# Sixteen weight tiles of a hybrid decoder layer: their low parts made by accumulating DMAs in place of VectorE subtractions

## The chip, the cores and the metric

The kernel runs on one core of one Trainium2 chip. The metric is the device time of one execution in microseconds, as the median of its runs; less is better. Engines are named as in the profile: PE (TensorE matmul), PEld (TensorE weight load), DVE (VectorE), ACT (ScalarE), POOL (GpSimd) and SP (SyncE). POOL and SP matter here as queues that issue DMAs: POOL's DMAs run on the queue that the profile calls q0 software_dynamic, SP's on q1 hardware_dynamic.

## What is computed

One layer of a decoder trunk for 512 positions and a model width of 1024, in float32:

```
u = RMSNorm(x);  z = u @ w_in            # columns: MoBA q,k,v | mLSTM q,k | mLSTM v | output gate | i,f gates | branch gates A, B
A = block-sparse causal attention (8 heads x 64)
B = chunkwise mLSTM (4 heads x 128), normalised, times sigmoid(output gate)
m = sigmoid(z_gA) * (A @ w_proj_a) + sigmoid(z_gB) * (B @ w_proj_b)
x = x + m @ w_out
x = x + SwiGLU(RMSNorm(x)) @ w_down;  out = RMSNorm(x)
```

Two families of weights are touched here: the branch gate B columns of w_in (called "gb") and the two projections w_proj_a and w_proj_b (called "p").

## The kernel before, in words

All products are made in three matmul passes, to keep float32 accuracy on a faster reduced format (float32r). A weight tile w is split into a high part h, which is w rounded to float32r, and a low part l = w - h. The same is done to the activations. Then h·h, l·h and h·l are accumulated in PSUM (`mm3`, lines 194 to 203): three matmuls for each 128 rows of depth, so 24 for one tile of 128 by 1024.

The weights ahead of the feed-forward part come as 60 such tiles, in the order of the table `UNITS`: q, k, v and mLSTM tiles first, then numbers 28 to 35 "ga" (branch gate A), 36 to 43 "gb" (branch gate B), 44 to 51 "p" (the projections, A and B rows side by side) and 52 to 59 "wo" (w_out). The helper `fill` takes the next tile and issues its matmuls, and between tiles the code issues the matmuls of attention and mLSTM. Two helpers prepare the tiles:

- `load_pair` (line 180) issues the loads of two tiles on SP's queue into buffers "raw" (pool tag R, 7 buffers; two of these hold activations until the last gb tile is done, so 5 rotate).
- `split_unit` (line 188) takes one raw tile and calls `split_hl` (line 157): ACT rounds it into "wh" (line 148) and DVE subtracts into "wl" (line 161). Both buffers come from pool tag W (10 buffers, two of them held as above). A raw buffer is free after the subtraction, a W buffer after the last matmul of its tile.

`fill` keeps the splits two tiles ahead of the matmuls. After the first stage the order of instructions on each engine is set by the scheduler that builds the program, from priorities and its own estimates; every engine then runs its list strictly in order, and each queue issues its DMAs in order.

Three more pieces come up later. The projections' outputs wait in 3 PSUM buffers "mm"; those of ga and gb are taken out by DVE (`run_g`, line 575), and the next tile that gets the same buffer can't start before that. The mLSTM part loads, for each of its 4 heads, a tile "R" of decay rows from DRAM on POOL's queue (`ml_load`, line 1370); DVE (line 1382) and ACT work on it next. And the feed-forward part issues 22 accumulating loads on POOL's queue (`gu_load`, line 705), which add DRAM data to a tile in SBUF, and 32 accumulating stores to DRAM (line 921).

The functions that the change touches, and what calls them:

Of the kernel before, what the change touches and what calls it, by code (L numbers as in the profile page):

```python
# [9 lines left out]
F32R = mybir.dt.float32r  # L10
BF16 = mybir.dt.bfloat16
AF = mybir.ActivationFunctionType
ALU = mybir.AluOpType
# [37 lines left out]
def _unit_order():  # L51

    u = []
    u += [("q", 0), ("q", 1), ("k", 0), ("k", 1), ("q", 2), ("q", 3)]
    u += [("va", 0), ("va", 1), ("va", 2), ("va", 3), ("k", 2), ("k", 3)]
    u += [("ob", 0), ("ob", 1)]
    u += [("vb", i) for i in range(4)]
    for h in (0, 2):
        u += [("qkb", h), ("qkb", 4 + h), ("qkb", h + 1), ("qkb", 5 + h)]
    u += [("ob", 2), ("ob", 3)]  # L60
    u += [("ga", m) for m in range(8)]
    u += [("gb", m) for m in range(8)]
    u += [("p", m) for m in range(8)]
    u += [("wo", m) for m in WO]
    return u


UNITS = _unit_order()
# [16 lines left out]
def hybrid_layer_kernel(ctx: ExitStack, tc, xT, wall, wgu, wds, wdl, g3v, vecs, wgates, consts, rope, out):  # L85
    nc = tc.nc
# [12 lines left out]
    def nm(p="t"):  # L99
        cnt[0] += 1  # L100
        return f"{p}{cnt[0]}"

    def slot(dt=F32, name="a"):
        return act.tile([P, S], dt, name=nm(name), tag="A")
# [4 lines left out]
    def blk(dt=F32, name="b", raw=False):  # L109
        t = dict(tag="R", bufs=NR) if raw else dict(tag="W", bufs=NW)  # L110
        return act.tile([P, 2 * S], dt, name=nm(name), **t)
# [16 lines left out]
    f = lambda t: t.bitcast(F32)  # L128
# [6 lines left out]
    def table(set_id):  # L135
        if ph["set"] == set_id:
            return
        with ExitStack() as es:
            for i in ph["ins"]:
                es.enter_context(tc.issue_after(i))  # L140
            ld = A.add_instruction(
                mybir.InstLoadActFuncSet(name=nc.get_next_instruction_name(), act_func_set_id=set_id)
            )
        ph.update(set=set_id, load=raw_ins(ld), ins=[])

    def act_(out_, in_, func, **kw):
        if func not in SETS:
            return A.activation(out_, in_, func, **kw)  # L148
        table(SETS[func])
        if ph["manual"]:  # L150
            return A.activation(out_, in_, func, **kw)
        with tc.issue_after(ph["load"]):
            i = A.activation(out_, in_, func, **kw)
        ph["ins"].append(raw_ins(i))
        return i

    def split_hl(src, name="h", dst=None):

        h, l = dst or (slot(F32R, name + "h"), slot(F32R, name + "l"))
        act_(h, src, AF.Copy)  # L160
        V.tensor_tensor(l, src, f(h), op=ALU.subtract)  # L161
        return h, l
# [11 lines left out]
    raw = {}  # L174
    whl = {}
# [4 lines left out]
    def load_pair():  # L180
        p = wstate["pair"]
        if p * 2 >= NU:
            return
        for u in (2 * p, 2 * p + 1):
            raw[u] = blk(name="raw", raw=True)
            nc.sync.dma_start(raw[u], wall[u])
        wstate["pair"] += 1

    def split_unit():
        u = wstate["split"]  # L190
        wstate["split"] += 1
        whl[u] = split_hl(raw.pop(u), dst=(blk(F32R, "wh"), blk(F32R, "wl")))
        if u % 2 == 1:
            load_pair() if u < NGEN - 4 else st["load"]()

# [33 lines left out]
    wstate["pair"] = 2  # L229
    wstate["split"] = 4  # L230
    load_pair()
    con = cst.tile([P, NC_], F32, name="con")
    nc.sync.dma_start(con, consts)
# [43 lines left out]
    for k in range(KT):  # L277
        if k < 4:
            t = blk2(F32R, "u", raw=k < 2)
            h, l = t[:, 0, :], t[:, 1, :]  # L280
        else:
            h, l = slot(F32R, "uh"), slot(F32R, "ul")
        wh, wl = w0h[k // 4][:, k % 4], w0l[k // 4][:, k % 4]
        halves = [(0, 1), (2, 3)] if k == 0 else [range(4)]
        c = slice(0, P * len(halves[0]))
        split_hl(t0[k // 4][:, k % 4, c], dst=(wh[:, c], wl[:, c]))
        act_(h, xs[k], AF.Copy, scale=col(G1 + k))
        V.scalar_tensor_tensor(l, xs[k], col(G1 + k), f(h), op0=ALU.mult, op1=ALU.subtract)
        uh.append(h)
        ul.append(l)  # L290

        for js in halves:
            if js[0]:
                c = slice(2 * P, S)
                split_hl(t0[0][:, 0, c], dst=(wh[:, c], wl[:, c]))
            for n, (w, r) in enumerate(((wh, h), (wl, h), (wh, l))):
                for j in js:
                    T.matmul(ps0[j], w[:, j * P : (j + 1) * P], r, start=k == 0 and n == 0, stop=k == KT - 1 and n == 2)  # L298
        if k:
            add_sq(1, xs[k - 1], k - 1)  # L300
        if k == KT - 4:
            load_pair()
        if k >= KT - 3:
            split_unit()
        if k == KT - 2:
            split_gw()
# [58 lines left out]
    def fill(n=1, mid=None):  # L365

        for _ in range(n):
            u = pos[0]
            if u >= len(UNITS):
                if mid:  # L370
                    mid()
                return
            while wstate["split"] <= min(u + LOOK, NGEN - 1):
                split_unit()
            pos[0] += 1
            kind, i = UNITS[u]
            g = run[kind](i, *whl.pop(u))
            next(g, None)
            if mid:
                mid()  # L380
            for _ in g:
                pass
# [1006 lines left out]
    def ml_a(h, b):  # L1389
        qh, ql = qkm[h]  # L1390
        kh, kl = qkm[4 + h]
        res = []
        for i in ((0, 1), (2,))[b]:
            ps = mmb() if i == 1 else sb()
            w = rbc[h][i]
            n = w.shape[-1]
            for j in range(4):
                if KR[j][0] == i:
                    c = slice(j * P, (j + 1) * P)
                    o = ps[:, KR[j][1]]  # L1400
                    T.matmul(o, kh[:, c], qh[:, j * P :], start=True, stop=False)
                    T.matmul(o, kl[:, c], qh[:, j * P :], start=False, stop=False)
                    T.matmul(o, kh[:, c], ql[:, j * P :], start=False, stop=True)
            V.scalar_tensor_tensor(w, ps[:, :n], sc_b, w, op0=ALU.mult, op1=ALU.mult)
            h_, l_ = slot(F32R, "Ah"), slot(F32R, "Al")
            res.append(split_hl(w, dst=(h_[:, :n], l_[:, :n])))

        w0, w1, w2 = rbc[h][0:3]
        if b == 0:
            V.tensor_tensor(w0[:, P:], w0[:, P:], w1, op=ALU.add)  # L1410
        else:
            V.tensor_tensor(w0[:, 2 * P :], w0[:, 2 * P :], w2[:, 0:256], op=ALU.add)
            V.tensor_tensor(w0[:, 3 * P :], w0[:, 3 * P :], w2[:, 256:384], op=ALU.add)
            res.append(split_hl(w0, "D"))
        return res, lambda: None
# [72 lines left out]
    while n < len(steps) or qa or qb:  # L1488
        if qa and (len(qa) >= LA or n >= len(steps)):
            kind, h, b, r = qa.pop(0)  # L1490
            qb.append((kind, h, b, moba_b(h, b, r) if kind == "a" else r, n))
        if n < len(steps):
            kind, h, b = steps[n]
            while kind == "b" and not (h in wready and h in qkm and 4 + h in qkm):
                advance()
            r, second = moba_a(h, b) if kind == "a" else ml_a(h, b)
# [22 lines left out]
        while qb and (qb[0][4] <= n - LC):  # L1519
            kind, h, b, r, _ = qb.pop(0)  # L1520
# [115 lines left out]
```

## Time and profile before

| what | value |
| --- | --- |
| median of 3 runs | 733.04 us (733.04 to 733.22) |
| profiled execution, first to last instruction (span) | 730.5 us |
| median less this span: what lies around it (the page gives no other time of its own for the profiled execution) | 2.5 us |
| PE busy | 721.6 us (99% of the span) |
| DVE busy | 618.7 us (85%) |
| ACT busy | 430.6 us (59%) |
| POOL busy | 64.6 us (9%) |
| granted TensorE clock, mean | 0.996 |

The profile is one execution, taken by the hardware profiler. Times inside it count from the first instruction. A row of a group of instructions has the busy time, the mean duration of one, and the idle time of the engine just before them with what ended it. PE's matmuls are pipelined, so the start of the next matmul tells more than the end of one.

### The profile page before, as it was taken

What the parts mean: (1) busy time and instruction counts of PE and PEld (TensorE: products, weight loads), DVE (VectorE), ACT (ScalarE), POOL (GpSimd) and SP (SyncE); (2) the same over time, 40 slices, a digit from 0 to 9 for tenths busy, and PEclk for the clock granted to TensorE, in tenths of its full rate; (3) what the DMA queues carried; (4) which work ended last, traced back from release to release, by engine and by line L of the source; (5) the groups of instructions that cost most, each with busy time, mean ns of one, the idle gap of its engine ahead of it and who ended that gap; (6) DMA issues with size and microseconds to landing.
All of it is one profiled execution on the core that took longest, in us unless ns stands there. A gap on an engine that the chain in (4) does not pass through costs nothing.

```text
span 730.5 us, 11386 instructions
## 1 busy us (share of the span) xinstructions
PE 721.6 (99%) x4191; PEld 636.7 (87%) x4191; DVE 618.7 (85%) x1106; ACT 430.6 (59%) x748; POOL 64.6 (9%) x87
## 2 busy tenths in 40 slices
PE   9999999999999999999999999999999999999995
PEld 6788888888888888888888998999899899899984
DVE  6998877899987669566788999899899899989996
ACT  6635776668846339523456656665655565655554
POOL 0004010000000000000000000400310310130000
PEclk9999999999999999999999999999999999999998
DMA  8778673232431222534767353975895795696403
GB/s 308 280 229 222 186 214 118 73 131 91 162 136 58 87 87 87 173 112 118 190 175 208 121 160 95 237 220 131 207 266 144 173 273 161 150 247 203 151 0 117
DMA packets 51320, 118.74 MB, mean 163 GB/s; under 512 B 5292, under 2 KB 9780, under 8 KB 51264
## 3 DMA queue, kind: packets, MB, share of 16 engines
q1 hardware_dynamic: 37024, 88.82, 35.9%
q0 software_dynamic: 9728, 26.80, 19.2%
q10 hardware_dynamic: 4512, 2.39, 1.1%
q8 instruction: 33, 0.54, 0.3%
q14 instruction: 23, 0.19, 0.1%
HBM read 101.17 MB, written 16.82 MB: 162 GB/s over the span
## 4 chain that ended last, share of the span: by engine, by line
PE 98%; DVE 0%; DMA 0%; issue 0%; ACT 0%; SPq 0%
PE mm L201 12%; PE mm L202 12%; PE mm L203 12%; PE mm L795 6%; PE mm L796 6%; PE mm L797 6%; PE s L795 3%; PE s L797 3%; PE s L796 3%; PE mm L904 3%; PE mm L905 2%; PE mm L906 2%; PE acc L1351 2%; PE mm L298 2%; PE mm L479 2%; PE mm L480 2%
## 5 line engine op out<-in xcount | busy, mean ns | idle before, releaser
L148 ACT ACTIVATE wh<-raw 128x1024 fp32r<-128x1024 f32 x56 | 59.2, 1058 | 77.7 <-PE mm L202 73.5
L795 PE MATMUL mm<-bq,w 128*128 128x256 f32 x264 | 75.6, 286 | 0.0
L796 PE MATMUL mm<-bq,w 128*128 128x256 f32 x264 | 74.9, 284 | 0.0
L797 PE MATMUL mm<-bq,w 128*128 128x256 f32 x264 | 74.8, 283 | 0.0
L161 DVE TENSOR_TENSOR wl<-raw,wh 128x1024 fp32r<-128x1024 f32 x56 | 68.1, 1219 | 6.4 <-ACT wh L148 5.5
L743 DVE TENSOR_TENSOR w<-s,w 128x1024 fp32r<-128x1024 f32 x44 | 53.6, 1218 | 8.4 <-ACT w L148 8.4
L148 ACT ACTIVATE w<-s 128x1024 fp32r<-128x1024 f32 x44 | 46.5, 1056 | 14.5 <-PE mm L202 5.4
L148 ACT ACTIVATE w<-raw 128x1024 fp32r<-128x1024 f32 (+2 forms) x48 | 46.1, 963 | 12.7 <-PE s L796 3.3
L705 POOL DMA_DIRECT2D s<-in_wgu_dram x22 | 19.0, 865 | 368.5 <-DVE ga L597 131.8
L795 PEld LDWEIGHTS mm<-bq,w 128*128 128x128 f32 x264 | 50.6, 192 | 0.7 <-ACT s L148 0.3
L796 PEld LDWEIGHTS mm<-bq,w 128*128 128x128 f32 x264 | 50.6, 192 | 0.3 <-issue 0.2
L797 PEld LDWEIGHTS mm<-bq,w 128*128 128x128 f32 x264 | 50.6, 192 | 0.1
L201 PE MATMUL mm<-u,wh 128*128 128x512 f32 x128 | 50.4, 394 | 0.0
L202 PE MATMUL mm<-u,wl 128*128 128x512 f32 x128 | 50.1, 391 | 0.0
L203 PE MATMUL mm<-u,wh 128*128 128x512 f32 x128 | 50.0, 391 | 0.0
L797 PE MATMUL s<-bq,w 128*128 128x256 f32 x176 | 49.8, 283 | 0.0
L202 PE MATMUL mm<-uh,wl 128*128 128x512 f32 x128 | 49.8, 389 | 0.0
L201 PE MATMUL mm<-uh,wh 128*128 128x512 f32 x128 | 49.8, 389 | 0.0
L203 PE MATMUL mm<-ul,wh 128*128 128x512 f32 x128 | 49.8, 389 | 0.0
L795 PE MATMUL s<-bq,w 128*128 128x256 f32 x176 | 49.8, 284 | 0.0
L796 PE MATMUL s<-bq,w 128*128 128x256 f32 x176 | 49.8, 283 | 0.0
L148 ACT ACTIVATE w<-sw 128x1024 fp32r<-128x1024 f32 x20 | 21.2, 1059 | 22.2 <-DVE sw L782 20.2
(404 smaller groups left out, 2238.2 us busy)
## 6 DMA issues: line engine op xcount, KB each, us to landing
raw<-in_wall_dram SPq DMA_DIRECT2D x56, 512.0 KB, 4.1
s<-in_wgu_dram SPq DMA_DIRECT2D x22, 512.0 KB, 4.8
s<-in_wgu_dram POOLq DMA_DIRECT2D x22, 512.0 KB, 5.9
raw<-in_wgu_dram SPq DMA_DIRECT2D x22, 512.0 KB, 5.2
raw<-in_wds_dram SPq DMA_DIRECT2D x20, 512.0 KB, 5.5
w<-in_wgu_dram SPq DMA_DIRECT2D x22, 256.0 KB, 6.8
h1d<-s POOLq DMA_DIRECT2D x16, 256.0 KB, 8.7
R<-scr POOLq DMA_DIRECT2D x4, 896.0 KB, 4.7
```

The lines of the kernel that those rows point to most:

```text
L148: return A.activation(out_, in_, func, **kw)
L161: V.tensor_tensor(l, src, f(h), op=ALU.subtract)
L201: T.matmul(ps, wh[:, c], rh[j], start=start and j == 0, stop=False)
L202: T.matmul(ps, wl[:, c], rh[j], start=False, stop=False)
L203: T.matmul(ps, wh[:, c], rl[j], start=False, stop=stop and j == n - 1)
L298: T.matmul(ps0[j], w[:, j * P : (j + 1) * P], r, start=k == 0 and n == 0, stop=k == KT - 1 and n == 2)
L705: nc.gpsimd.dma_start(s13, wgu[i][:, 512:1536].rearrange("p (x c) -> p x c", x=2), accum_op=ALU.add)
L743: V.tensor_tensor(dst[1], src, f(dst[0]), op=ALU.subtract)
L795: T.matmul(ps, wh[:, c], bh, start=first and k == 0, stop=False, skip_group_check=not first)
L796: T.matmul(ps, wl[:, c], bh, start=False, stop=False, skip_group_check=not first)
L797: T.matmul(ps, wh[:, c], bl, start=False, stop=k == 3, skip_group_check=not first)
L904: T.matmul(ps, bh, wh[:, d], start=first and k == 0, stop=False, skip_group_check=not first)
```

## The change

For the eight gb tiles, the load moves from SP to POOL and writes a float32r tile, so that the transfer itself rounds ("rawh", in the R buffers); this is used as the high part. ACT writes the negated high part into wl, and a second DMA on POOL adds the same weights from DRAM to it. For the eight p tiles, the load stays on SP; ACT makes the high part and, in a second pass, the negated one, and a DMA on POOL adds the raw tile from SBUF to that. The 16 subtractions on DVE are gone. The other tiles are as before. Line numbers from 193 on move by 19.

```diff
--- before
+++ after
@@ load_pair @@
         for u in (2 * p, 2 * p + 1):
-            raw[u] = blk(name="raw", raw=True)
-            nc.sync.dma_start(raw[u], wall[u])
+            kind = UNITS[u][0]
+            if kind == "gb":
+                raw[u] = blk(F32R, "rawh", raw=True)
+                nc.gpsimd.dma_start(raw[u], wall[u])
+            else:
+                raw[u] = blk(name="raw", raw=True)
+                nc.sync.dma_start(raw[u], wall[u])
@@ split_unit @@
-        whl[u] = split_hl(raw.pop(u), dst=(blk(F32R, "wh"), blk(F32R, "wl")))
+        kind = UNITS[u][0]
+        if kind == "gb":
+            h, l = raw.pop(u), blk(F32R, "wl")
+            act_(l, f(h), AF.Copy, scale=-1.0)
+            nc.gpsimd.dma_start(l, wall[u], accum_op=ALU.add)
+            whl[u] = h, l
+        elif kind == "p":
+            r, h, l = raw.pop(u), blk(F32R, "wh"), blk(F32R, "wl")
+            act_(h, r, AF.Copy)
+            act_(l, r, AF.Copy, scale=-1.0)
+            nc.gpsimd.dma_start(l, r, accum_op=ALU.add)
+            whl[u] = h, l
+        else:
+            whl[u] = split_hl(raw.pop(u), dst=(blk(F32R, "wh"), blk(F32R, "wl")))
```

The scheduler puts the instructions into a new order. The first place is POOL's list in the mLSTM stage: R is the tile of decay rows, one for each of the four heads, in_wall_dram holds the weight tiles, and s is a tile of the feed-forward part. Before:

```order
L1370 DMA R_1765<-scr 128x1792
L1370 DMA R_2048<-scr 128x1792
L1370 DMA R_2125<-scr 128x1792
L1370 DMA R_2288<-scr 128x1792
L705 DMA s_3563<-in_wgu_dram 128x1024
```

After the change:

```order
L1389 DMA R_2125<-scr 128x1792
L188 DMA rawh_2464<-in_wall_dram 128x1024
L188 DMA rawh_2466<-in_wall_dram 128x1024
L188 DMA rawh_2575<-in_wall_dram 128x1024
L1389 DMA R_2288<-scr 128x1792
L188 DMA rawh_2577<-in_wall_dram 128x1024
L188 DMA rawh_2679<-in_wall_dram 128x1024
L202 DMA wl_2626<-in_wall_dram 128x1024
```

The loads of the first three gb tiles now stand between the third and the fourth R load, on the same queue.

The second place is POOL's list further down, with the accumulating transfers (line 202 for gb, 208 for p) of the last gb tiles and the first p tiles; there was nothing here before:

```order
L188 DMA rawh_2681<-in_wall_dram 128x1024
L202 DMA wl_2880<-in_wall_dram 128x1024
L188 DMA rawh_2793<-in_wall_dram 128x1024
L202 DMA wl_2920<-in_wall_dram 128x1024
L188 DMA rawh_2795<-in_wall_dram 128x1024
L202 DMA wl_2954<-in_wall_dram 128x1024
L208 DMA wl_2995<-raw_2883 128x1024
L208 DMA wl_3032<-raw_2885 128x1024
L208 DMA wl_3069<-raw_2957 128x1024
```

The loads of gb tiles 5, 6 and 7 alternate with accumulating transfers, each of which waits for ACT.

The third place is ACT's list at the end of the mLSTM stage (ri, ob and yb belong to the mLSTM output, sqh to its norm, ga and gb are the gates). Before:

```order
L148 ACTIVATE sqh_2779<-sqn_2772 128x512
L148 ACTIVATE wh_2885<-raw_2683 128x1024
L148 ACTIVATE wh_2926<-raw_2797 128x1024
L153 ACTIVATE ri_2864<-d_2667 128x512
L153 ACTIVATE ri_2864<-ri_2864 128x512
L153 ACTIVATE ri_2877<-d_2773 128x512
L153 ACTIVATE ri_2877<-ri_2877 128x512
L141 ACT_TABLE_LOAD
```

After the change:

```order
L148 ACTIVATE sqh_2776<-sqn_2769 128x512
L148 ACTIVATE wl_2880<-rawh_2681 128x1024
L148 ACTIVATE wl_2920<-rawh_2793 128x1024
L153 ACTIVATE ri_2859<-d_2666 128x512
L153 ACTIVATE ri_2859<-ri_2859 128x512
L153 ACTIVATE ri_2872<-d_2770 128x512
L148 ACTIVATE wl_2954<-rawh_2795 128x1024
L153 ACTIVATE ri_2872<-ri_2872 128x512
L141 ACT_TABLE_LOAD
L153 ACTIVATE ob_942<-ob_942 128x512
L153 ACTIVATE ob_1040<-ob_1040 128x512
L153 ACTIVATE ob_2131<-ob_2131 128x512
```

The negations of gb tiles 5, 6 and 7 (wl from rawh) stand ahead of the table load and of the passes over the p tiles. Behind these rows come the fourth ob pass, one yb pass, one ga pass, and then the two passes over p tile 0, with one more yb pass between them. PE's list of matmuls is the same as before, row by row. DVE's keeps its order around lines 1382 and 575: the removal of ga's PSUM tile still stands right behind the four instructions on R.

## Rows read from the trace of the kernel before

**Rows 1.** The profile page: the busy time of each engine, and the chain of work that ended last, by engine.

```profile
PE 721.6 (99%) x4191; PEld 636.7 (87%) x4191; DVE 618.7 (85%) x1106; ACT 430.6 (59%) x748; POOL 64.6 (9%) x87
...
PE 98%; DVE 0%; DMA 0%; issue 0%; ACT 0%; SPq 0%
```

**Rows 2.** Busy time of each engine by stretch: from the last mLSTM tiles to the end of the p tiles. Columns: the stretch and its length, then busy time and number of instructions of PE, PEld, DVE, ACT and POOL, then the granted clock, DMA share and GB/s.

```profile
205.00:256.00 51.00, 51.00 (x244) 43.13 (x243) 38.45 (x63) 23.11 (x39) 0.53 (x1) 1.00 0.29 101
256.00:301.60 45.60, 45.60 (x206) 37.84 (x205) 34.11 (x48) 27.62 (x43) 0.00 (x0) 1.00 0.32 105
301.60:345.20 43.60, 43.60 (x194) 36.11 (x193) 28.64 (x38) 14.80 (x17) 0.89 (x1) 1.00 0.42 131
```

**Rows 3.** All that PE waited for in the whole span, from the list of waits (total, times, longest).

```profile
PE s L217 <- DVE zero L214: 1.2, 1, 1.2
```

**Rows 4.** Groups of instructions by line from 230 to 330 us: the subtractions on DVE, the rounding on ACT, the removal of the gb tiles from PSUM.

```profile
L161 DVE TENSOR_TENSOR wl<-raw,wh 128x1024 fp32r<-128x1024 f32 x17 | 20.7, 1219 | 1.6 <-ACT wh L148 1.6
...
L148 ACT ACTIVATE wh<-raw 128x1024 fp32r<-128x1024 f32 x18 | 19.1, 1059 | 42.4 <-PE mm L202 41.8 <-PE mm L203 0.7
```

**Rows 5.** The timeline at the start of ga tile 3: DVE's four instructions on the fourth R tile and the removal of a ga tile, then PE's own weight load and matmul; POOL's row is the issue of that R load.

```profile
213.76 0.53 POOL L1370 DMA_DIRECT2D R<-scr  x1 [29.53 <-DVE wl L161]
...
219.24 1.14 DVE L1382 SCALAR_TENSOR_TENSOR R<-con,cS,R 128x128 f32<-128x128 f32 x4 [1.87 <-DMA R<-scr]
220.30 0.68 DVE L575 TENSOR_TENSOR ga<-mm,rn 128x512 f32<-128x512 f32 x1
...
220.99 0.34 PE L1403 MATMUL mm<-qk 128*128 128x384 f32 x1
221.03 0.19 PEld L201 LDWEIGHTS mm<-u,wh 128*128 128x128 f32 x1
221.17 0.40 PE L201 MATMUL mm<-u,wh 128*128 128x512 f32 x1
```

**Rows 6.** The four R loads: duration of the issue on POOL in ns (min/median/max), and time from issue to landing in us (min/median/max).

```profile
L1370 POOL DMA_DIRECT2D R<-scr x4: 528/542/558, 145.4 to 213.8; - x4
...
DMA to landing us min/median/max: 4.5/4.7/5.5
```

**Rows 7.** The DMA queues from 213 to 219.5 us (6.5 us): packets, MB, and the time that their packets took as a share of 16 engines' stretch; then the two transfers with size and time to landing.

```profile
q0 software_dynamic: 144, 0.92, 33.9%
q1 hardware_dynamic: 144, 0.52, 24.7%
issues: line engine op xcount, KB each, median us to landing
R<-scr POOLq DMA_DIRECT2D x1, 896.0 KB, 5.5
raw<-in_wall_dram SPq DMA_DIRECT2D x1, 512.0 KB, 3.3
```

**Rows 8.** The same from 336.5 to 342 us (5.5 us), where one accumulating load of 512 KB runs on POOL's queue.

```profile
q0 software_dynamic: 144, 0.52, 56.7%
```

**Rows 9.** The 22 accumulating loads of the feed-forward part: issue on POOL in ns, time to landing in us (both min/median/max).

```profile
L705 POOL DMA_DIRECT2D s<-in_wgu_dram x22: 850/869/888, 336.0 to 657.0; - x22
...
DMA to landing us min/median/max: 5.2/5.9/9.1
```

**Rows 10.** The 32 accumulating stores to DRAM, from SBUF: issue on POOL for the first group, and landing of all.

```profile
L921 POOL DMA_DIRECT2D h1d<-s x16: 859/1059/1571, 457.0 to 642.1; - x16
...
DMA to landing us min/median/max: 6.3/9.2/12.9
```

**Rows 11.** The loads of weight tiles on SP from 255 to 297 us: time to landing in us (min/median/max).

```profile
DMA to landing us min/median/max: 3.1/3.2/3.3
```

**Rows 12.** ACT's timeline, three roundings that waited for a W buffer (the end of gb tiles 0, 1 and 2) and the passes that stand between the last of them and p tile 0.

```profile
261.50 1.06 ACT L148 ACTIVATE wh<-raw 128x1024 fp32r<-128x1024 f32 x1 [1.94 <-PE mm L202]
...
268.13 1.06 ACT L148 ACTIVATE wh<-raw 128x1024 fp32r<-128x1024 f32 x1 [4.08 <-PE mm L202]
273.57 1.06 ACT L148 ACTIVATE wh<-raw 128x1024 fp32r<-128x1024 f32 x1 [4.38 <-PE mm L202]
...
277.96 0.63 ACT L153 ACTIVATE ri<-ri 128x512 f32<-128x512 f32 x1
278.61 1.28 ACT L141 ACT_TABLE_LOAD   x1
279.90 1.15 ACT L153 ACTIVATE ob<-ob 128x512 f32<-128x512 f32 x2
...
281.91 1.14 ACT L153 ACTIVATE ob<-ob 128x512 f32<-128x512 f32 x2
```

**Rows 13.** The 32 matmuls of the p tiles that read A's output and the high part (four to each tile): duration in ns, first and last start in us.

```profile
L201 PE MATMUL mm<-ya,wh x32: 389/389/389, 301.7 to 341.8; 128*128 128x512 f32 x32
```

## The prediction

> **What bounds the kernel now.** I read the page first: PE is busy for 99% of the span and makes up 98% of the chain that ended last, while DVE, which the change relieves, has 85% and no share of that chain [rows 1]. A share of the whole span can hide a stage with another limit, so next came the table by stretch for the time in which the 16 tiles are made and used: PE has no idle time in any of its three rows, DVE is at 66 to 75% and ACT at 34 to 61% [rows 2]. The list of waits says it once more: in the whole span PE waited for another engine once, for 1.2 us at the start, far from here [rows 3]. So a tile that is ready earlier gains nothing; a tile that is ready too late costs its whole lateness, once, since nothing behind it has idle time that could take it up. A result within 0.2% of 733.04 (1.47 us) is what I call no change, as a measurement of this kernel can tell little less.
>
> **What is removed.** Sixteen subtractions of 1.22 us each [rows 4], 19.5 us of DVE. DVE was idle for only 1.6 us before the whole group of 17, so it made them while PE worked on other tiles; their worth on the path is 0. The cover is PE's list of matmuls, which is the same before and after.
>
> **What is added.** ACT gets one more pass for each p tile: 8 x 1.06 = 8.5 us [rows 4]; for gb the negation takes the place of the rounding. ACT idled 42 us before this group, nearly all of it waiting for PE to free a buffer, so the passes are hidden where they don't have to wait. POOL gets 24 DMAs: 8 loads at 0.53 us of issue [rows 6] and 16 accumulating ones at 0.87 [rows 9], 18 us in a stretch where it issued one. SP loses 8 loads. The question is thus whether any tile comes late, and whether the new DMAs make another one late. Two places have to be worked out.
>
> **Place 1, the fourth R load.** In POOL's new list the loads of gb tiles 0 to 2 stand ahead of the R load of the fourth head. Before, that load was issued at 213.76 and DVE sat idle until 219.24 for it; behind the four instructions on R stands the removal of a ga tile from PSUM, which ended at 220.98. PE's weight load for the next ga tile, the one that needs this buffer, began at 221.03, and its matmul followed the one before without a gap [rows 5]. So there is no slack: each us that R lands later is a us of PE. The load of gb tile 2 needs a raw buffer that becomes free at 213.76 too (the release that the POOL row names), so it is issued then, and R behind it. Least delay: only the issue of the new load, 0.53, and R then lands as fast as the fastest R load, 4.5 [rows 6]: 218.8, earlier than before, which gains nothing because PE is still on its earlier matmuls; 0. With the issue and the 5.45 that R took beside SP's load of the same size: 214.29 + 5.45 = 219.74, 0.5 late. With both transfers in one queue, back to back: R alone takes 4.7, and the 512 KB ahead of it take 24.7% of 6.5 us = 1.6 us of 16 engines [rows 7]: 213.76 + 4.7 + 1.6 = 220.06, 0.85 late. I take 0.7, between the last two, because these are the very transfers in question [rows 7] and only the queue differs. The worst case needs a slower transfer and is the first rival.
>
> **Place 2, the tiles themselves.** PE starts p tile 0 at 301.7, and eight p tiles take 5.44 us each (301.7 to 341.8 spans seven tiles and nine matmuls of 0.227) [rows 13]; counted back, gb tiles 5, 6 and 7 start at 285.4, 290.8 and 296.3. For gb the raw buffer now stays taken until PE is done with the tile, so with five rotating, tile 5 loads when tile 0 is done, 261.5, tile 6 at 268.1, tile 7 at 273.6 [rows 12].
> - gb 5: load 4.7 (an R load, the nearest without accumulation on POOL), negation 1.06, accumulation 5.9 [rows 4, 6, 9]: ready at 273.2, 12 us early.
> - gb 6: from 268.2, behind the issue for tile 5: 279.9, 11 us early.
> - gb 7: POOL is in order, so its load waits for the negation of tile 6 (274.0) and the issue of that accumulation: 274.9 + 4.7 + 1.06 + 5.9 = 286.6, nearly 10 us early.
> - p 0: its buffer is free when gb tile 3 is done, 279.9, and the load takes 3.2 [rows 11], but ACT's list holds the negation of gb 7 (till 280.7), then one Exp, the table load and four ob passes, 0.6 + 1.3 + 2.3 [rows 12], a yb and a ga pass at half of an ob pair, 0.57 each; p 0's two passes with one between end at 288.5. Accumulated at 294.4, 7.5 us early.
> - p 2: the tightest. In the built program its raw load waits for the accumulation of p 0, whose buffer it takes: 294.4 + 3.2 + 2 x 1.06 + 5.9 = 305.6, against 312.8; 7 us early. The accumulation counts twice, so this holds up to (312.8 - 288.5 - 5.3) / 2 = 9.5 us for each.
> An accumulation from SBUF into SBUF is not in the trace. The accumulating loads (512 KB, 5.2 to 9.1) are its nearest [rows 9], and at these the p tiles cost 0; the accumulating stores (256 KB, up to 12.9) are the far end [rows 10], the second rival. The first wo tile starts at 301.7 + 8 x 5.44 = 345.2, 40 us after the accumulation of p 2 has freed a raw buffer; 0.
>
> **Sum.** 0 - 0 + 0.7 + 0: 731.2 for the profiled execution with its 730.5, and, with the 2.5 us around it, 733.7 for the median of 733.04.
>
> **The rivals.**
> - *The rounding load is slow.* The load of gb tile 2 changes the type, float32 to float32r, and no transfer before does. If its packets take as long as those of an accumulation, the 512 KB ahead of R cost 56.7% of 5.5 us = 3.1 us [rows 8] and R lands at 221.56, 2.35 us late: 735.4, slower. For it: both leave the plain copy. [...] It decides from 1.47 us, that is about 2.2 us of data ahead of R. 20%. [...]
> - *Late p tiles.* At 12.9 us for each accumulation, p 2 comes 2 x (12.9 - 9.5) = 6.8 us late: 740.5. For it: those stores read SBUF, too [rows 10]. Against it: those queue up six at a time and write DRAM; the stretch of the p tiles has a DMA share of 0.42 [rows 2]. 7%.
> - *DVE holds up POOL's issue.* If an issue on POOL had to wait for the DVE instruction that runs, the longest being a subtraction of 1.22 us, R would be 0.7 + 1.2 = 1.9 late: 734.9. The 22 issues of the accumulating loads lie between 0.850 and 0.888 us beside a busy DVE [rows 9]; only the issues of the stores are stretched, by up to 0.7 [rows 10]. 5%. [...]
> - *DVE is the limit after all.* Then 19.5 us would go: 713.5. Against it: a PE without idle time [rows 2, 3]. 2%.
> Should the load not round at all, low parts would be zero and no time would differ.
>
> **How the numbers follow.** The forecast has 64%, the rivals 20, 7, 5 and 2, and 2 are left for a small gain that I don't see. Forecast and first rival give 84%: from no delay with some spread, 732.8, to 735.4 with some, 735.8. Faster 0.04, within 0.2% 0.64, slower 0.32.
>
> **What would show it.** Right: PE idle once, 0.3 to 1 us, at the start of a ga tile near 221, released by DVE; R landing 6 to 6.5 us after the first load's issue; no wait of PE for a DMA into wl; DVE's share near 82%. The first rival: the same gap at over 1.5 us. The second: PE waiting for an accumulation near 312. The third: POOL issues of over 1 us in this stretch. A gap of PE at any other place would prove the account of the slack wrong.

## The result and the profile after

The changed kernel takes 740.45 us (median; four runs, 739.74 to 742.61) against 733.13 for the kernel before (four runs, 733.04 to 733.28). The ratio is 1.0102, with a 95% interval of 1.0090 to 1.0114. Measured again, five rounds on another chip: 739.94 against 733.12, ratio 1.0091 (1.0078 to 1.0104). So it is slower by 7 us; the forecast was 733.7, in a range up to 735.8. The profiled execution is one of those at 740.45; its span is 738.6 us, 8.1 more than before. The numbers of the runs below leave out one execution, of e8, which took 1519.7 us for no reason that the record shows.

The page after, engines and chain [rows 1]:

```profile
PE 724.3 (98%) x4191; PEld 638.5 (86%) x4191; DVE 601.0 (81%) x1090; ACT 437.9 (59%) x756; POOL 82.6 (11%) x111
...
PE 81%; issue 8%; DVE 4%; DMA 4%; ACT 2%; POOL 1%; POOLq 0%; ACTq 0%; SPq 0%
```

DVE has 16 instructions fewer, as the diff says, and 17.7 us less work (19.5 were forecast), and that bought nothing. PE's share of the chain fell from 98% to 81%: something else now ends last, somewhere. The table by stretch says where, the list of PE's waits says how often [rows 2, 3]:

```profile
205.00:256.00 51.00, 50.29 (x242) 42.29 (x241) 35.41 (x61) 24.66 (x40) 7.48 (x11) 1.00 0.52 122
256.00:301.60 45.60, 45.60 (x206) 37.94 (x205) 24.90 (x41) 23.72 (x37) 5.93 (x8) 1.00 0.46 114
301.60:345.20 43.60, 39.39 (x168) 32.19 (x167) 19.91 (x29) 23.61 (x29) 5.70 (x7) 0.96 0.92 255
```

```profile
PE mm L220 <- DVE ga L614: 4.2, 1, 4.2
PE s L236 <- DVE zero L233: 1.2, 1, 1.2
PE mm L220 <- DVE ga L594: 0.7, 1, 0.7
```

PE is idle in two places. The 0.7 us is the forecast gap near 221. The 4.2 us is in the stage of the p tiles, which I had put at 0; there the granted clock is 0.96 instead of 1.00, and the DMA share 0.92 instead of 0.42. No wait of PE for a DMA is in the list: no low part came late.

The matmuls of PE come in the same order in both traces, so each can be paired with itself, and the difference of the two starts shows where the time went: 0.6 us in the first microseconds of the kernel (the other profiles below have 0.0 to 0.9 there, with no relation to their edits), 0.86 at 221, then 0.1 up to the p tiles, 4.37 at one matmul there, 1.5 over the eight behind it, 0.6 after PE's last matmul.

**The gap at 221** [rows 5]. POOL, DVE and PE, each a timeline:

```profile
214.64 0.53 POOL L188 DMA_DIRECT2D rawh<-in_wall_dram  x1 [5.82 <-DVE wl L161]
215.25 0.53 POOL L1389 DMA_DIRECT2D R<-scr  x1
...
220.84 1.14 DVE L1401 SCALAR_TENSOR_TENSOR R<-con,cS,R 128x128 f32<-128x128 f32 x4 [2.87 <-DMA R<-scr]
221.90 0.68 DVE L594 TENSOR_TENSOR ga<-mm,rn 128x512 f32<-128x512 f32 x1
...
222.64 0.50 PE L220 MATMUL mm<-u,wh 128*128 128x512 f32 x1 [0.71 <-DVE ga L594]
```

R is issued 0.61 us behind the load of gb tile 2, lands 5.6 us later, and everything behind it moves with it. The mechanism and the size are those of the forecast.

**The gap in the p stage.** Three names are needed. The p stage leaves one merged tile "mg" for each p tile; like the weights it is split, by ACT into mgh (L148) and by DVE into mgl (L161). On DVE's list, L614, which takes the first half of p tile 1 out of PSUM, stands behind mgl of p tile 0, and PE needs that PSUM buffer for the second half of p tile 2. First SP, then ACT's list without a line left out, then DVE and PE:

```profile
305.97 0.33 SPq L191 DMA_DIRECT2D raw<-in_wall_dram  x1
```

```profile
309.14 1.04 ACT L148 ACTIVATE wl<-raw 128x1024 fp32r<-128x1024 f32 x1
312.99 1.06 ACT L148 ACTIVATE wh<-raw 128x1024 fp32r<-128x1024 f32 x1 [2.80 <-DMA raw<-in_wall_dram]
313.95 0.61 ACT L153 ACTIVATE ga<-ga 128x512 f32<-128x512 f32 x1
314.47 1.04 ACT L148 ACTIVATE wl<-raw 128x1024 fp32r<-128x1024 f32 x1
315.42 0.61 ACT L153 ACTIVATE gb<-gb 128x512 f32<-128x512 f32 x1
316.05 1.28 ACT L141 ACT_TABLE_LOAD   x1
317.35 1.06 ACT L148 ACTIVATE wh<-raw 128x1024 fp32r<-128x1024 f32 x1
318.31 1.04 ACT L148 ACTIVATE wl<-raw 128x1024 fp32r<-128x1024 f32 x1
319.26 0.61 ACT L148 ACTIVATE mgh<-ga 128x512 fp32r<-128x512 f32 x1
```

```profile
319.90 0.69 DVE L161 TENSOR_TENSOR mgl<-ga,mgh 128x512 fp32r<-128x512 f32 x1 [9.56 <-ACT mgh L148]
320.51 0.68 DVE L614 TENSOR_TENSOR ga<-mm,ga 128x512 f32<-128x512 f32 x1
```

```profile
316.65 0.39 PE L222 MATMUL mm<-ya,wh 128*128 128x512 f32 x1
321.25 0.79 PE L220 MATMUL mm<-yb,wh 128*128 128x512 f32 x1 [4.21 <-DVE ga L614]
321.84 0.63 PE L221 MATMUL mm<-yb,wl 128*128 128x512 f32 x1
322.27 0.63 PE L222 MATMUL mm<-yb,wh 128*128 128x512 f32 x1
```

Read it from the end. PE waits for L614, which waits behind mgl, which waits for mgh of p tile 0. Its input was ready since 310.33, but ACT took it up only at 319.26: ahead of it in ACT's list stand the passes over p tiles 4 and 5, and the first of these waited until 312.9 for its raw tile. That tile's load was issued at 305.97, the moment when the accumulation of p tile 1, which held the raw buffer, had landed. Two transfers are in this chain (the accumulation of p 1, issued at 298.09, and the load of p 4; size and time to landing):

```profile
wl<-raw POOLq DMA_DIRECT2D x1, 512.0 KB, 7.8
...
raw<-in_wall_dram SPq DMA_DIRECT2D x1, 512.0 KB, 6.9
```

Before, the roundings of p tiles 4 and 5 stood ahead of that mgh as well. But p 4's load was issued at 285.55 and had landed at 288.8, 13 us before ACT rounded it and 20 us before that mgh, and ACT waited for nothing but PE and DVE. The load by SP, its time to landing, then ACT's roundings of p tiles 4 and 5 and mgh:

```profile
285.55 0.33 SPq L186 DMA_DIRECT2D raw<-in_wall_dram  x1
...
raw<-in_wall_dram SPq DMA_DIRECT2D x1, 512.0 KB, 3.3
...
301.68 1.06 ACT L148 ACTIVATE wh<-raw 128x1024 fp32r<-128x1024 f32 x1 [2.11 <-PE mm L202]
...
307.12 1.06 ACT L148 ACTIVATE wh<-raw 128x1024 fp32r<-128x1024 f32 x1 [2.50 <-PE mm L202]
308.80 0.63 ACT L148 ACTIVATE mgh<-ga 128x512 fp32r<-128x512 f32 x1 [0.62 <-DVE ga L597]
```

The last three PE rows show how the other 1.5 us come about: behind the gap the matmuls start 0.43 us apart instead of 0.23, until about 324.

So the theory to test (A): p tile 4 is loaded too late, since the gb tiles hold the raw buffers longer and the accumulations of the p tiles hold them on; ACT, in order, is late at mgh of p tile 0. Rivals: the accumulated low parts themselves are late (B, the second rival of the prediction); the DMA traffic as such costs, by slower transfers or by PE's clock (C). In the expectations of e1 and e2, B stands for the gb half as the only cause.

### The profile page after: what moved, and what is told of

It is laid out like the page before. It is cut to its first block, busy times and chain, and to the rows that moved or that the text cites. A ratio compares the mean times of both kernels' runs of the same rounds, so it can differ in the third digit from the quotient of the medians.

```text
span 738.6 us, 11408 instructions
## 1 busy us (share of the span) xinstructions
PE 724.3 (98%) x4191; PEld 638.5 (86%) x4191; DVE 601.0 (81%) x1090; ACT 437.9 (59%) x756; POOL 82.6 (11%) x111
## 4 chain that ended last, share of the span: by engine, by line
PE 81%; issue 8%; DVE 4%; DMA 4%; ACT 2%; POOL 1%; POOLq 0%; ACTq 0%; SPq 0%
PE mm L220 7%; PE mm L222 7%; PE mm L221 7%; PE mm L814 6%; PE mm L815 6%; PE mm L816 6%; PE s L814 3%; PE s L816 3%; PE s L815 3%; PE mm L923 2%; PE mm L924 2%; PE mm L925 2%; PE mm L317 2%; PE mm L498 2%; PE mm L499 1%
## 5 line engine op out<-in xcount | busy, mean ns | idle before, releaser
L148 ACT ACTIVATE wh<-raw 128x1024 fp32r<-128x1024 f32 x48 | 50.7, 1057 | 54.5 <-PE mm L221 40.5
L148 ACT ACTIVATE w<-s 128x1024 fp32r<-128x1024 f32 x44 | 46.5, 1056 | 14.5 <-PE mm L221 5.4
L148 ACT ACTIVATE w<-raw 128x1024 fp32r<-128x1024 f32 (+2 forms) x48 | 46.2, 964 | 11.9 <-PE s L815 3.3
L161 DVE TENSOR_TENSOR wl<-raw,wh 128x1024 fp32r<-128x1024 f32 x40 | 48.7, 1221 | 4.2 <-ACT wh L148 3.3
L220 PE MATMUL mm<-u,wh 128*128 128x512 f32 x96 | 38.1, 397 | 0.7 <-DVE ga L594 0.7
L222 PE MATMUL mm<-u,wh 128*128 128x512 f32 x96 | 37.6, 392 | 0.0
L220 PE MATMUL mm<-uh,wh 128*128 128x512 f32 x96 | 37.4, 389 | 0.0
L222 PE MATMUL mm<-ul,wh 128*128 128x512 f32 x96 | 37.4, 389 | 0.0
L148 ACT ACTIVATE w<-sw 128x1024 fp32r<-128x1024 f32 x20 | 21.2, 1060 | 22.1 <-DVE sw L801 20.1
```

The costliest lines, as they stand in the source:

```text
L220: T.matmul(ps, wh[:, c], rh[j], start=start and j == 0, stop=False)
L222: T.matmul(ps, wh[:, c], rl[j], start=False, stop=stop and j == n - 1)
```

## The experiments

Ratios are to the kernel before, run on the same chip, with their 95% intervals. e1 to e4 shared one chip (before: 732.79), a1 and e5 to e7 another (733.12); e8 ran on a third (733.20).

**e1, the gb half alone.** The branch for p is removed from `split_unit`, so that these tiles are made as before:

```diff
-        elif kind == "p":
-            ...
-            nc.gpsimd.dma_start(l, r, accum_op=ALU.add)
-            whl[u] = h, l
```

> Only the gb half of the change (rounding loads and accumulations on POOL); the eight p tiles are made as before, by ACT rounding and a DVE subtraction. Theory A (the loss near 320 comes from the p half: ACT's new passes over p tiles 4 and 5 stand ahead of the mgh pass of p tile 0 and wait for a late load): no wait of PE near 315 to 321, what is left is the late fourth R load, about 0.9 us: some 734.0. Rival B (POOL's new gb traffic and the raw buffers that gb keeps longer are the cause, the p half only shows it): a wait of 3 us or more stays in the p stage, 737 or more. Rival C (the extra DMA traffic as such costs, through the clock or PE's rows): half the traffic, about half the loss, some 736.8.

732.85 us, ratio 1.0012 (1.0000 to 1.0023): no wait in the p stage, which speaks against B and C as this expectation puts them. The single runs spread widely, 732.4 to 736.7, and the profile is of the slowest. It shows one wait, at 221, of 2.3 us, and this load of R:

```profile
R<-scr POOLq DMA_DIRECT2D x1, 896.0 KB, 7.2
```

In the last 2 us of that load the mean busy share of the 16 DMA engines (second number from the right, columns as in [rows 2]) is 0.12, what two of the 16 give; from 215 to 219.8 it is 0.76:

```profile
219.80:221.90 2.10, 1.97 (x11) 1.44 (x9) 0.00 (x0) 0.48 (x1) 0.00 (x0) 1.00 0.12 48
```

**e8, the same kernel again**, for a profile of another execution.

> The gb half alone once more, for a second profile: eight of twelve executions of it lay at 732.4 to 732.9, as the kernel before, four at 734.2 to 736.7, and the profile was of one of the four, with R landing 7.2 us after its issue and a wait of PE of 2.3 us. If the lateness of the fourth R load makes the difference between executions, a profile at about 732.7 shows R landing 5.5 us after its issue or sooner and a wait of PE of at most 0.7 us near 221; a profile at 734 or more shows R at over 6 us and a wait of over 1 us there.

733.36 against 733.20, ratio 1.0001 (0.9990 to 1.0013). The profile is of a run at 732.89, with

```profile
R<-scr POOLq DMA_DIRECT2D x1, 896.0 KB, 5.1
```

and a wait of 0.3 us at 221; in the p stage PE waits for nothing here either. (Of e1's eight executions that this expectation puts at 732.4 to 732.9, one lies at 733.4.) So one and the same program loses there 0.3 or 2.3 us, as R takes 5.1 or 7.2 us to land.

**e2, the p half alone.**

```diff
-            if kind == "gb":
+            if kind == "none":
```

(in both helpers).

> Only the p half of the change (negated pass on ACT and an accumulation from SBUF for the eight p tiles); the gb tiles are made as before. Theory A: ACT's list has the passes of p tiles 4 and 5 ahead of mgh of p tile 0 here too, and p tile 4's load waits for an accumulation; the R load is on time, so the gap at 221 is gone (0.9 less). How much of the 4.4 us wait near 320 stays says how much of the lateness the gb half brings along: with accumulations as slow as in the changed kernel (4.7 to 9.9 us) and raw buffers that gb frees early, I expect a smaller wait, 1 to 4 us: 734 to 738, say 736. Rival B (gb's part is the cause): no wait in the p stage, 733.1. Rival C (traffic as such): half of the loss, 736.8, without a single large wait of PE.

732.48 us, ratio 0.9997 (0.9988 to 1.0005), no wait of PE from the gb tiles on. I had expected a wait of 1 to 4 us, as the accumulations would be slow; they are (4.6 to 11.1 us, median 8.7, against 8.2 in the changed kernel), but p tile 4 was loaded at 286.3, ahead of all of them. Taken alone this is the result that the expectation gives to B; e1 excludes the gb half as the only cause. Each half is harmless alone: the loss is in their meeting.

**e3, p accumulated from DRAM**, so that a raw buffer is free after ACT's second pass:

```diff
-            nc.gpsimd.dma_start(l, r, accum_op=ALU.add)
+            nc.gpsimd.dma_start(l, wall[u], accum_op=ALU.add)
```

> As the changed kernel, but the accumulations of the p tiles read the tile again from DRAM instead of the raw buffer in SBUF, as those of gb do; so a raw buffer is free after ACT's second pass and no load of a later p tile waits for an accumulation. Theory A: p tile 4's load starts some 8 us earlier, ACT is not late at mgh of p tile 0, the wait of 4.2 us near 320 goes and the slow clock behind it: 740.45 - 4.4 - 1.6 = about 734.5. If the accumulations themselves come too late for PE (my second rival of the prediction, B), they would do so here as well, at 5 to 10 us each: 738 or more, with PE waiting for an accumulation. Rival C (traffic as such): no better than the changed kernel, 740.5, as the bytes moved are the same.

734.46 us, ratio 1.0025 (1.0017 to 1.0034). The wait in the p stage is gone, though each accumulation takes still longer, 8.1 to 11.7 us (median 9.8). Apart from where the accumulations read, only the times at which buffers come free differ. That speaks for A, and against B and C. ACT's list, in the order of the changed kernel, with the load of p tile 4 landed at 306.8:

```profile
311.21 1.06 ACT L148 ACTIVATE wh<-raw 128x1024 fp32r<-128x1024 f32 x1
312.18 1.04 ACT L148 ACTIVATE wl<-raw 128x1024 fp32r<-128x1024 f32 x1
313.12 0.62 ACT L148 ACTIVATE mgh<-ga 128x512 fp32r<-128x512 f32 x1
```

mgh is 6.1 us earlier than in the changed kernel, and that is early enough.

**e4, mgh first.** ACT's passes over p tile k are tied behind mgh of p tile k - 4; transfers and buffers as in the changed kernel:

```diff
-            act_(h, r, AF.Copy)
+            m = UNITS[u][1]
+            with ExitStack() as es:
+                if m >= 4:
+                    es.enter_context(tc.issue_after(st["mgi"][m - 4]))
+                act_(h, r, AF.Copy)
...
-        mgd.append(split_hl(ga, "mg"))
+        h, l = slot(F32R, "mgh"), slot(F32R, "mgl")
+        st.setdefault("mgi", []).append(raw_ins(act_(h, ga, AF.Copy)))
+        V.tensor_tensor(l, ga, f(h), op=ALU.subtract)
+        mgd.append((h, l))
```

> As the changed kernel, with all its transfers, but in ACT's list the two passes over p tile k (k from 4 on) stand behind the mgh pass of p tile k - 4, so that mgh doesn't wait for the load of a later p tile. Theory A: mgh of p tile 0 is on time, the PSUM buffer is freed on time and the wait near 320 goes; p tile 4 is made later, but PE needs it only near 323; if that is too tight a smaller wait for p tile 4 or 5 comes in its place. 734.5 to 737. Rival B (the low parts come late themselves): the passes are now later still, so the wait gets longer, 741 or more, and PE waits for an accumulation. Rival C (traffic as such): 740.5, unchanged.

734.01 us, ratio 1.0023 (1.0014 to 1.0033). mgh of p tile 0 starts at 312.29, the long wait is gone, and a short one for an accumulation has come in its place:

```profile
PE s L240 <- DVE zero L237: 1.2, 1, 1.2
PE mm L225 <- DMA wl<-raw: 0.6, 1, 0.6
PE mm L224 <- DVE ga L598: 0.4, 1, 0.4
```

The passes over p 4 now come later than in the changed kernel's list, the tiles are accumulated as slowly, and yet 6 us are back: it was the order on ACT that PE waited for. The 0.6 shows how near B was by then: the accumulation of p tile 3 landed at 319.64, and PE wanted it 0.6 us before.

**a1, the changed kernel again.**

> The changed kernel itself, unaltered, as the yardstick for the runs beside it. All theories: about 740, with runs between 739.5 and 743, and in the profile one wait of PE of 4 us or more for the DVE instruction that frees a PSUM buffer of the p stage, with about 1.6 us of matmuls at a slower clock behind it.

739.94 us (738.36 to 740.72), with waits of 3.0 and 0.7 us; I had expected 4 us or more for the first. The long wait varies from execution to execution (4.2 in the first profile).

**e5, R on SP's queue.**

```diff
-        nc.gpsimd.dma_start(t, scr[h : h + 1, :].partition_broadcast(P))
+        (nc.sync if h == 3 else nc.gpsimd).dma_start(t, scr[h : h + 1, :].partition_broadcast(P))
```

> As the changed kernel, but the fourth R load is issued by SP's queue, where no load of a gb tile stands ahead of it. If the prediction's first place was right (R stands behind the load of gb tile 2, 0.86 us in the profile) the gap of PE near 221 goes and the rest stays: 740.2 - 0.9 = 739.3, with the wait of 4 us near 320 as before. If R was late for another reason (the two transfers share the 16 engines, whichever queue issues them), the gap stays: 740.2.

739.32 us, ratio 1.0077 (1.0062 to 1.0092). R lands at 218.1, 4.5 us after its issue, and the load of gb tile 2 beside it at 219.5; the gap at 221 is gone and the long one is left (4.8 us in this profile). The difference to a1, 0.6 us, is within what these runs tell; that the wait at 221 comes from R's place on POOL's queue is shown by the profile.

**e6, both cures** (the edits of e4 and of e5).

> As the changed kernel, with both cures: the fourth R load on SP's queue, and ACT's passes over p tile k behind the mgh pass of p tile k - 4. Theory A: both waits gone, at most the 0.6 us wait for the accumulation of p tile 3 is left, 732.8 to 733.6, and no single runs at 736 to 738 any more, since those came from an R load that landed still later. Rival C (the extra traffic costs something by itself): what remains above the kernel before is over 1.5 us, 734.3 or more. A gain over the kernel before (under 732) is expected by none.

732.61 us (732.00 to 733.12), ratio 0.9993 (0.9984 to 1.0001). PE waits for nothing after the start, no run is at 736 any more, and all 16 low parts are made by DMAs. The stage of the p tiles:

```profile
301.60:330.00 28.40, 28.40 (x127) 23.50 (x127) 12.58 (x19) 20.29 (x26) 5.14 (x6) 1.00 1.01 275
```

The DMA engines are busy throughout these 28 us (share 1.01), PE has no idle time and its clock is whole: this ends rival C, by which the traffic costs something by itself. e6 differs from e4 in R's queue alone, and the ratio goes from 1.0023 to 0.9993; so what e4 had left came with R's place on POOL's queue.

**e7, gb with a high part of its own.** The gb tiles are loaded by SP as plain float32 (`kind == "none"` in `load_pair`), and ACT writes both parts, so that a raw buffer is free after two passes and not when PE is done with the tile:

```diff
-            h, l = raw.pop(u), blk(F32R, "wl")
-            act_(l, f(h), AF.Copy, scale=-1.0)
+            r, h, l = raw.pop(u), blk(F32R, "wh"), blk(F32R, "wl")
+            act_(h, r, AF.Copy)
+            act_(l, r, AF.Copy, scale=-1.0)
             nc.gpsimd.dma_start(l, wall[u], accum_op=ALU.add)
```

> All 16 low parts by accumulating transfers, as in the changed kernel and with the same bytes moved, but the gb tiles are loaded by SP as plain float32 and ACT writes the rounded part into a block of its own; so a raw buffer of a gb tile is free after ACT's two passes, not when PE is done with the tile. The p tiles are coded as in the changed kernel, with the same order of ACT's list around mgh of p tile 0. Theory A with held buffers (the p loads come late because gb tiles keep raw buffers until PE has used them): p tile 0 is loaded and accumulated some 5 us earlier or more, mgh of p tile 0 is on time, no wait in the p stage: 732.8 (R is on time as well). Rival C (it is the traffic of 16 accumulations that slows the loads): the wait of 4 us near 320 stays, 738 or more.

732.73 us, ratio 0.9995 (0.9987 to 1.0004). With the same 16 accumulations, the p tiles' own in 5.4 to 12.0 us (median 8.2), the loss is gone. p tile 4 is loaded at 283.4, 23 us earlier than in the changed kernel, and mgh follows the two passes over p tile 5 at once:

```profile
307.52 1.06 ACT L148 ACTIVATE wh<-raw 128x1024 fp32r<-128x1024 f32 x1 [1.61 <-PE mm L222]
308.48 1.05 ACT L148 ACTIVATE wl<-raw 128x1024 fp32r<-128x1024 f32 x1
309.43 0.61 ACT L148 ACTIVATE mgh<-ga 128x512 fp32r<-128x512 f32 x1
```

All profiles side by side (us, from the traces). In ACT's list the passes over p tiles 4 and 5 stand ahead of mgh of p tile 0 in all but the last two:

| kernel | p tile 4 landed | mgh of p tile 0 starts | longest wait of PE in the p stage |
| --- | --- | --- | --- |
| e7 | 287.0 | 309.4 | 0 |
| before | 288.8 | 308.8 | 0 |
| e2 | 289.4 | 309.7 | 0 |
| e8 | 300.7 | 309.5 | 0 |
| e1 | 304.3 | 313.4 | 0 |
| e3 | 306.8 | 313.1 | 0 |
| a1 | 311.4 | 317.7 | 3.0 |
| e5 | 312.0 | 318.4 | 4.8 |
| changed | 312.9 | 319.3 | 4.2 |
| e6 (mgh first) | 311.4 | 311.7 | 0 |
| e4 (mgh first) | 311.9 | 312.3 | 0 (0.6 for an accumulation) |

(In e1's profile PE comes to the p tiles 4.5 us later than before, after its wait at 221.) In the changed kernel and in e3, a1 and e5 mgh starts 6.3 to 6.4 us behind the landing: that is ACT's list between the two. In e3 the load is early enough for that. Where the load is early or the list is changed, the wait is gone. Theory A stands. No version beats the kernel before: e2, e6 and e7 all equal it, as a PE without waits is the bound in each.

## Why the prediction was wrong

- **What bounds the kernel.** Right: PE. Taking up to 17.7 us off DVE gave nothing in any version; the rival "DVE is the limit" is out.
- **Place 1.** Right in mechanism and size. Forecast 0.7, measured 0.86 and 0.81 by the paired matmuls of the two profiles of the changed kernel; in e3, e4 and e8 it was 0.4 to 0.55, in one execution of e1 2.4. The rounding load is nearly as quick as a plain one: gb tiles 0 to 2 took 3.7, 4.8 and 4.0 us to land, against 3.4, 4.5 and 3.3 on SP before (all eight: 3.6 to 6.7, median 4.1). So the first rival's reason, twice the time, is out, though R itself can land 2 us later than usual. Why it does so in some executions stays open: a profile shows one execution, and in e1's only the load of gb tile 2 ran with R, and landed at 218.0, long before R at 222.3. That profile shows how, not why: the last 2 us of R were moved by two engines' worth of the 16.
- **Place 2 is the step that failed.** It set out to show that each tile is ready in time, and the tiles were: PE never waited for one in the changed kernel. What it left out is the rest of ACT's list. It called ACT's passes "hidden where they don't have to wait", and then followed only how long p 0 and p 2 themselves take. It didn't ask which instruction of another chain is queued behind the passes that wait: mgh of p tile 0, from which PE's PSUM buffer hangs. And it followed the raw buffers to p 2 ("its raw load waits for the accumulation of p 0") but not two tiles on, where the load of p 4 waits for the accumulation of p 1 in the same way.
- **The terms of Place 2, one by one.** The terms for p 0 add up to 288.7, not 288.5, which changes nothing. The load of gb tile 7 was issued at 278.0 (forecast 274.9) and took 6.7 us instead of 4.7, beside an accumulation; p 0 was accumulated at 298.3 instead of 294.4. For p 2 the table gave 305.6; it was 312.7, on a PE that ran 1.5 us later, so the 7 us of slack were all but used up: 312.7 against 314.4. The accumulations from SBUF, which I took at 5.9 us, needed 4.7 to 9.9, median 8.2, and the plain loads of the p tiles 4.4 to 10.2 where I took 3.2 [rows 11]. Durations of a quiet stretch [rows 2] were used for a stretch that the change itself fills, from a DMA share of 0.42 to 0.92.
- **"A tile that is ready too late costs its whole lateness, once".** Wrong: the 4.4 us cost 1.5 more, through the clock (last section).
- **The second rival** gave 740.5, near the measured time, with a chance of 7%. Its reason holds in part (slow accumulations from SBUF), its mechanism doesn't: it had PE wait for an accumulation at p 2. With these slow accumulations e2, e6 and e7 lose nothing; that its number fits is chance.
- **DVE holding up POOL's issues:** out. The 16 accumulations took 0.848 to 0.888 us to issue in the changed kernel, as those of before [rows 9]. During 12 of these issues DVE worked, and they took 0.848 to 0.888; during the other four it did not, and they took 0.853 to 0.856.
- **What would show it.** "A gap of PE at any other place would prove the account of the slack wrong" was the right sentence, and it applied.

## What to carry to other kernels

When a change puts a transfer or a pass on an engine that runs its list in order (ACT here took up mgh 8.9 us after its input was ready), follow not only the data that it makes: write down the next instructions behind it on that engine, and for each buffer that it holds longer the load that gets the buffer next, until a chain reaches the bounding engine. Two halves that are each free can meet in one buffer pool and one list: here longer-held buffers made a load late, and that list made another chain wait for the load. And work out slack with durations of the stretch as it will be, not as it was; here p tile 4 took 6.9 us to load instead of 3.3, as the DMA share of the stretch of the p tiles went from 0.42 to 0.92.

## What the runs showed of the hardware

- **The longer gaps of PE cost more than themselves.** After gaps of 2.3 us (e1), 3.0 (a1), 4.2 (changed) and 4.8 (e5), 8, 8, 7 and 14 matmuls started about 0.43 us apart instead of 0.23, which cost another 1.7, 1.7, 1.5 and 3.0 us by the paired matmuls. After gaps of 0.3 to 0.7 us there was none of it. The slow stretch did not always start at once: in e1 four matmuls ran at full pace first:

```profile
224.06 0.50 PE L214 MATMUL mm<-u,wh 128*128 128x512 f32 x1 [2.29 <-DVE ga L588]
224.40 0.39 PE L215 MATMUL mm<-u,wl 128*128 128x512 f32 x1
...
225.48 0.63 PE L216 MATMUL mm<-u,wh 128*128 128x512 f32 x1
225.91 0.63 PE L214 MATMUL mm<-u,wh 128*128 128x512 f32 x1
...
228.04 0.63 PE L216 MATMUL mm<-u,wh 128*128 128x512 f32 x1
228.47 0.43 PE L214 MATMUL mm<-uh,wh 128*128 128x512 f32 x1
```

  The granted clock had the same stretch: it was 0.50 for 3.41 us in e1, a1 and the changed kernel, and for 6.83 us in e5 (its mean from 301.6 to 330 us is 0.94 in a1 and 0.88 in e5). So in these four profiles the price went with this time, 1.5 to 1.7 us for 3.41 and 3.0 for 6.83, while gaps of 2.3 to 4.2 us had the same 3.41. In e1, the 3.41 us before it falls and those behind (columns as in [rows 2]: PE's busy time stands first, the clock third from the right):

```profile
221.72:225.13 3.41, 1.12 (x6) 0.89 (x6) 2.86 (x8) 2.42 (x6) 0.00 (x0) 1.00 0.02 5
225.13:228.54 3.41, 3.41 (x10) 2.65 (x9) 1.64 (x2) 0.43 (x1) 0.53 (x1) 0.50 0.02 4
```

  In the 3.41 us before the fall PE was busy for 1.12 us in e1. In a1 three matmuls started at full pace behind the gap, from 319.72 on, and the slow ones began at 320.52, 0.8 us later; in the changed kernel PE was idle for the whole 3.41 us before the fall (317.40 to 320.81), and the fall came 0.44 us before its next matmul. What sets the moment of the fall and the length of the stretch, these runs do not show.
- **Accumulations from SBUF into SBUF** (512 KB) took 4.6 to 4.8 us with little or nothing beside them (4.7 for p tile 0 of the changed kernel, at a DMA share of 0.60) and up to 12 in a crowd (9.9 for the slowest of the changed kernel, at a share of 1.06; 12.0 in e7); those from DRAM took 5.3 to 6.6 in the changed kernel's gb stage and 8.1 to 11.7 in e3's p stage.
- **A load that changes the type** from float32 to float32r took 3.4 to 4.1 us in the quiet stretch from 224 to 235 us, over all profiles that have one there (3.6 in the changed kernel, issued at 231.7); a plain load on SP took 3.1 to 3.3 [rows 11].
- **Matmuls on plain float32 tiles.** In the kernel before, the four of 128x512 for the norms (L338, two pairs) took 0.592 to 0.672 us, and the two of a pair started 0.51 and 0.43 us apart. Those on float32r tiles took 0.389 [rows 13] and started 0.23 us apart.
